# Opening the tile context of a three-block sequence kernel with its other scheduling mode

## The chip, the cores and the metric

The program runs on one core of one Trainium2 chip. The metric is the device time of one execution in microseconds; the kernel before takes 3362.69 us (median of three runs, 3362.65 to 3365.91). The engines are TensorE (PE in the profile; its weight loads are PEld), VectorE (DVE), ScalarE (ACT), GpSimd (POOL) and SyncE (SP); each works through its own list of instructions, and semaphores order what the engines hand to each other.

## What is computed

Three blocks on a sequence of 512 tokens by 1024 channels, in fp32, one after the other, and each has a mixer and a feed-forward part. Cut to what matters:

```python
# block 1: four branches, gated and merged
y_sc   = (sc_b * causal_dwconv(sc_c * sc_x, sc_conv)) @ sc_out
y_pool = pool_mixer(pool_in, pool_w, pool_scale)
y_conf = conformer_conv(conf_in, ...)
y_diff = diff_attention(q, k, v, ...) @ diff_out
x = x + (sum of sigmoid(gate_b) * y_b) @ w_o
x = x + conv_glu_ffn(rms_norm(x, ffn_norm), ffn_up, ffn_conv, ffn_down)
# block 2: adaptive norms, gated delta rule (8 heads of 64) and RWKV-7 (8 heads of 64)
y_a = gated_deltanet(qkv, z, b, a, ...) @ w_branch_gdn
y_b = rwkv7_time_mix(p_b, ...)          @ w_branch_rwkv
x = x + gate1 * ((sigmoid(gl_a) * y_a + sigmoid(gl_b) * y_b) @ w_out)
x = x + gate2 * conv_glu(norm2(x), w_ffn_in, conv_ffn, w_ffn_out)
# block 3: adaptive norms, gated linear attention and a state-space scan, both in
# both directions, with states from a context of 256 tokens; then a SwiGLU
```

## The kernel before

The activations lie feature-major: a tile is 128 channels by 512 tokens, and the 1024 channels are eight such tiles. All large weights come as one stream of pieces of eight 128x128 blocks in the order of use (464 pieces). `load()` (L315 to 329) fetches a piece of 512 KB into `wr` on SP's queue and splits it into two parts for the fast fp32r product: `wh` on ScalarE (L325) and `wl` on VectorE (L326), each with three buffers. The activations `h` are split in the same way, so that one product of 128 channels is three matmuls of 128x512 for each 128 input channels: L364 (`h` high by `wh`), L365 (`h` low by `wh`) and L366 (`h` high by `wl`) in `lin()`; L350 to L352 in `product()` do the same for halves of the tokens and for the context. `lin()` accumulates in one of three PSUM banks with the tag `mm` (L243), and a bank comes free when its result has been read.

Who runs when is not written out by hand. Python traces the program once; a scheduler in the tile context sets the order of each engine's instructions from the traced order, the dependences and priorities. `z.first()` (L252 to 254) lifts what it holds by an offset of 4000 places: the weight loads and the steps that read a product out of its bank stand under it. So the weight products, which depend on nothing but the stream, lie between the steps of the recurrences.

The mixer of block 2 (`second()`) goes over four pairs j of heads. A pair's preparation takes r, k, v and q, k, v (made by `lins(j)`) through norms (`rstds()`: L602 logarithms and L605 exponentials, each with its own table load on ScalarE; sums by L613/L614), decays (L1323 to L1355), products among tokens (L1366, L1474, L1482; L1464 broadcasts a row of decays by a GpSimd DMA) and an inversion by levels (`invert()`, L676 to L736, with transposes at L652). Then come the two chains of chunks `rwkv()` and `gdn()`; L1421, L1422, L1428, L1437 and L1443 carry RWKV's state from chunk to chunk; L1230 to L1240 norm the results and store them in `yo`. Traced behind a pair are `lins(j + 1)` and some gates, whose tanh goes to the DRAM tensor `gt` (L944, L945). Two, one, one and twelve of the sixteen gates are traced with pairs 0 to 3:

```python
            for _, o in zip(range((2, 1, 1, 12)[j]), gates):
                aside(z, z.lin(h, "w_in_2", (4912 + P * o if o < 8 else 3888 + P * (o - 8))), gt, o)
```

After the last pair, L425 and L426 (`split()`) make the two parts of the eight results (the last pair's directly), and sixteen products over `yr` and `yg` follow (`w_branch_rwkv_2` and `w_branch_gdn_2`, four input tiles each, the fourth from the last pair).

The mixer of block 3 (`third()`) starts with gated linear attention: scans (L1292), states (L1746, L1748), and eight levels of scores (L1772 to L1778, cuts of differences and their exponentials). Beside it the columns of the state-space part are made by `ssd_col()` (L1938); `conv4()` (L1916 to L1930) reads a product out of its bank with one ScalarE instruction and three VectorE taps (L1926), after which the bank is free. The state-space stage itself follows (L1972 to L2083).

Each block and each feed-forward starts with a norm in two halves of 256 tokens (`Rms`): the sums per token by L498, Newton steps for the inverse root (L506 to L515, rows of 128x2), the factor spread by L541, and then for each of eight tiles L558, L565 and L566, which write the parts of `h`.

The tile context is opened in one line of `kernel()`, L2107.

## Time and profile before

| | |
|---|---|
| median of the runs | 3362.69 us |
| span of the profiled execution | 3361.9 us |
| TensorE busy | 3272.1 us (97%) |
| weight loads (PEld) busy | 2720.8 us (81%) |
| VectorE busy | 2235.4 us (66%) |
| ScalarE busy | 1495.8 us (44%) |
| GpSimd busy | 100.5 us (3%) |
| DMA | 393 MB, 117 GB/s in the mean |
| stages of the span | block 1 mixer to some 580 us, feed-forward to 960; block 2 mixer to 1615, feed-forward to 2000; block 3 mixer to 2980, feed-forward to 3362 |

The profiled execution's own time differs from the median by 0.8 us. Busy time counts the records of an engine; records of TensorE overlap, since a matmul's end is modelled and the next one starts before it. In the groups, "idle before" is the time the engine waited ahead of the instructions of a group, and behind the arrow stands what ended most of it.

### The profile page before, as it was taken

The page shows a single profiled execution, that of the slowest core. Times are in us where ns is not written, and L with a number is a line of the kernel's source. Part 1 is how long each engine was busy: PE and PEld are TensorE (multiplying, and loading weights), DVE is VectorE, ACT ScalarE, POOL GpSimd, SP SyncE. Part 2 cuts the span into 40 slices and gives each one's busy share as a digit, 9 for nine tenths or more (in the row PEclk, how much of TensorE's full clock was granted, in tenths as well). Part 3 has the DMA queues.
Part 4 walks back from the last instruction along what each step waited for, and adds up shares of the span by engine and source line. Part 5 has one row for each costly group of instructions (what it writes and reads, how often), then busy time and mean ns, then how long its engine had stood idle before and what let it go on. Part 6 is the DMA issues. An engine that isn't in the chain of part 4 may idle for free. (4 is left out here: it accounts for less than half of the span.)

```text
span 3361.9 us, 46572 instructions
## 1 busy us (share of the span) xinstructions
PE 3272.1 (97%) x18165; PEld 2720.8 (81%) x18165; DVE 2235.4 (66%) x3675; ACT 1495.8 (44%) x2491; POOL 100.5 (3%) x186
## 2 busy tenths in 40 slices
PE   7999999999999999999999999999999999999998
PEld 6778888888887887887888888888877777888886
DVE  4696645976578677666886558777687896363344
ACT  6443423432346656653432334555546665232221
POOL 0000000000000000000000000000000001000000
PEclk9999999999999999999999999999999999999999
DMA  3222233654332112215457223222227567323222
GB/s 133 70 69 94 92 122 101 219 194 153 103 102 77 51 44 76 68 49 176 132 183 236 94 82 128 73 78 94 78 88 232 165 210 235 126 89 99 94 95 75
DMA packets 128317, 393.22 MB, mean 117 GB/s; under 512 B 16056, under 2 KB 23480, under 8 KB 128096
## 3 DMA queue, kind: packets, MB, share of 16 engines
q1 hardware_dynamic: 113776, 346.82, 32.1%
q0 software_dynamic: 13168, 42.36, 3.7%
q8 instruction: 143, 2.34, 0.3%
q10 hardware_dynamic: 1152, 1.05, 0.1%
q14 instruction: 78, 0.64, 0.1%
HBM read 358.44 MB, written 31.74 MB: 116 GB/s over the span
## 5 line engine op out<-in xcount | busy, mean ns | idle before, releaser
L364 PE MATMUL mm<-h,wh 128*128 128x512 f32 x2400 | 947.2, 395 | 0.8 <-ACT t L944 0.7
L365 PE MATMUL mm<-h,wh 128*128 128x512 f32 x2400 | 947.5, 395 | 0.0
L366 PE MATMUL mm<-h,wl 128*128 128x512 f32 x2400 | 946.5, 394 | 0.0
L325 ACT ACTIVATE wh<-wr 128x1024 fp32r<-128x1024 f32 x464 | 490.7, 1059 | 976.0 <-PE mm L365 700.6
L326 DVE TENSOR_TENSOR wl<-wr,wh 128x1024 fp32r<-128x1024 f32 x464 | 567.2, 1223 | 477.3 <-ACT wh L325 472.2
L364 PEld LDWEIGHTS mm<-h,wh 128*128 128x128 f32 x2400 | 452.2, 188 | 97.7 <-issue 5.4
L366 PEld LDWEIGHTS mm<-h,wl 128*128 128x128 f32 x2400 | 452.3, 188 | 97.3 <-issue 6.0
L365 PEld LDWEIGHTS mm<-h,wh 128*128 128x128 f32 x2400 | 452.3, 188 | 96.2 <-issue 5.4
L364 PE MATMUL mm<-p,wh 128*128 128x512 f32 x599 | 236.8, 395 | 0.0
L365 PE MATMUL mm<-p,wh 128*128 128x512 f32 x599 | 236.5, 395 | 0.1
L366 PE MATMUL mm<-p,wl 128*128 128x512 f32 x599 | 236.5, 395 | 0.0
L350 PE MATMUL mm<-h,wh 128*128 128x256 f32 (+1 forms) x480 | 159.8, 344 | 14.3 <-DVE t L1926 5.5
L351 PE MATMUL mm<-h,wh 128*128 128x256 f32 (+1 forms) x480 | 159.9, 338 | 1.6 <-DVE h L566 1.6
L352 PE MATMUL mm<-h,wl 128*128 128x256 f32 (+1 forms) x480 | 158.7, 335 | 0.0
L301 DVE SCALAR_TENSOR_TENSOR ac<-wa,adas,ac 128x1024 f32<-128x1024 f32 x98 | 125.4, 1280 | 23.0 <-DMA wa<-wa 22.7
L365 PEld LDWEIGHTS mm<-p,wh 128*128 128x128 f32 x599 | 112.5, 188 | 27.5 <-DVE p L426 0.8
L366 PEld LDWEIGHTS mm<-p,wl 128*128 128x128 f32 x599 | 112.5, 188 | 26.9
L364 PEld LDWEIGHTS mm<-p,wh 128*128 128x128 f32 x599 | 112.5, 188 | 26.5
L350 PEld LDWEIGHTS mm<-h,wh 128*128 128x128 f32 x480 | 93.4, 199 | 25.3 <-ACT h L565 4.3
L351 PEld LDWEIGHTS mm<-h,wh 128*128 128x128 f32 x480 | 94.9, 199 | 9.8 <-DVE h L566 2.2
L352 PEld LDWEIGHTS mm<-h,wl 128*128 128x128 f32 x480 | 94.8, 199 | 8.4
L747 DVE SCALAR_TENSOR_TENSOR f<-mm,par,f 128x511 f32<-128x511 f32 (+1 forms) x128 | 95.4, 745 | 1.1
(661 smaller groups left out, 5288.1 us busy)
## 6 DMA issues: line engine op xcount, KB each, us to landing
wr<-w SPq DMA_DIRECT2D x464, 512.0 KB, 3.5
wa<-wa SPq DMA_DIRECT2D x96, 512.0 KB, 4.3
e<-cum SPq DMA_DIRECT2D x64, 256.0 KB, 5.4
x<-x POOLq DMA_DIRECT2D x40, 256.0 KB, 4.9
s<-ecum SPq DMA_DIRECT2D x64, 128.0 KB, 4.4
cd<-t POOLq DMA_DIRECT2D x24, 256.0 KB, 2.3
gt<-t POOLq DMA_DIRECT2D x16, 256.0 KB, 2.5
fr<-gt SPq DMA_DIRECT2D x16, 256.0 KB, 2.9
```

The source lines that it names most:

```text
L301: self.V.scalar_tensor_tensor(a, raw, s[:, k, m:m + 1], a, op0=ALU.mult, op1=ALU.add)
L325: self.A.activation(hi, raw, AF.Copy)
L326: self.V.tensor_tensor(lo, raw, hi.bitcast(F32), op=ALU.subtract)
L350: self.T.matmul(ps[:, n], lhsT=wh, rhs=x[0][k][:, n], start=k == 0, stop=False)
L351: self.T.matmul(ps[:, n], lhsT=wh, rhs=x[1][k][:, n], start=False, stop=False)
L352: self.T.matmul(ps[:, n], lhsT=wl, rhs=x[0][k][:, n], start=False, stop=k == last)
L364: self.T.matmul(out, lhsT=wh, rhs=x[0][k], start=k == 0, stop=False)
L365: self.T.matmul(out, lhsT=wh, rhs=x[1][k], start=False, stop=False)
L366: self.T.matmul(out, lhsT=wl, rhs=x[0][k], start=False, stop=k == last)
L747: z.V.scalar_tensor_tensor(out[:, d:], src[:, :S - d], w[:, n - 1 - d:n - d], out[:, d:], op0=ALU.mult, op1=ALU.add)
```

## The change

The context is opened in the mode in which the scheduler plays the program in time, with durations that it assumes for each instruction, and takes at each point what can run then, instead of ordering by places and priorities alone. Comments and docstrings were taken out as well, which leaves the numbers of the lines as they were. No other line differs.

```diff
-    with tile.TileContext(nc) as tc:
+    with tile.TileContext(nc, schedule_with_timeline_sim=True) as tc:
```

The instructions are the same on every engine but ScalarE, which has 67 table loads in place of 65; their order differs. Three places show it.

GpSimd, second block, before pair 3: `gt` is the store of a gate (L945), `ga2317` and `ga2332` are pair 3's two broadcasts, `yo` the store of pair 2's results. Before:

```order
L945 DMA gt1377_7561<-t2541_12418 128x512
L1464 DMA ga2317_11565<-gd1408_7776 128x512
L945 DMA gt1377_7561<-t2546_12452 128x512
L945 DMA gt1377_7561<-t2551_12486 128x512
L945 DMA gt1377_7561<-t2556_12520 128x512
L1235 DMA yo1378_7562<-ga2203_11019 128x512
L1240 DMA yo1378_7562<-ra2230_11125 128x512
L945 DMA gt1377_7561<-t2561_12554 128x512
L1464 DMA ga2332_11621<-gd1408_7776 128x512
L945 DMA gt1377_7561<-t2566_12588 128x512
```

After:

```order
L945 DMA gt1377_7561<-t2571_12622 128x512
L945 DMA gt1377_7561<-t2576_12656 128x512
L945 DMA gt1377_7561<-t2581_12690 128x512
L945 DMA gt1377_7561<-t2586_12724 128x512
L945 DMA gt1377_7561<-t2591_12758 128x512
L1464 DMA ga2317_11565<-gd1408_7776 128x512
L1235 DMA yo1378_7562<-ga2203_11019 128x512
L1240 DMA yo1378_7562<-ra2230_11125 128x512
L1464 DMA ga2332_11621<-gd1408_7776 128x512
```

Ahead of pair 3's first broadcast stand two of the twelve gates t2536 to t2591 before (t2536 is the row above these), and all twelve after.

TensorE, second block, pair 3's preparation: `g` and `r` are small banks of the two chains, L1474 and L1482 the products among tokens, `mm` the bank of a weight product over `h` (before) or over `yr` (after, the fill of the next stage). Before:

```order
L365 MATMUL mm2562_12557<-h894_4666,wh2554_12492 128x512
L366 MATMUL mm2562_12557<-h893_4665,wl2555_12493 128x512
L1474 MATMUL g2320_11579<-fg2277_11385 128x128 x4
L1482 MATMUL g2322_11589<-fg2271_11346,fg2277_11385 128x128 x4
L364 MATMUL mm2562_12557<-h895_4667,wh2554_12492 128x512
L365 MATMUL mm2562_12557<-h896_4668,wh2554_12492 128x512
L366 MATMUL mm2562_12557<-h895_4667,wl2555_12493 128x512
L364 MATMUL mm2562_12557<-h897_4669,wh2554_12492 128x512
```

After:

```order
L1319 MATMUL r2319_11573<-q1400_7730,lx2311_11541 128x512
L365 MATMUL mm2616_12808<-fg2597_12770,wh2584_12696 128x512
L366 MATMUL mm2616_12808<-fg2596_12769,wl2585_12697 128x512
L365 MATMUL mm2622_12831<-fg2597_12770,wh2584_12696 128x512
L366 MATMUL mm2622_12831<-fg2596_12769,wl2585_12697 128x512
L365 MATMUL mm2625_12848<-fg2597_12770,wh2589_12730 128x512
L366 MATMUL mm2625_12848<-fg2596_12769,wl2590_12731 128x512
L1474 MATMUL g2320_11579<-fg2277_11385 128x128 x4
L1482 MATMUL g2322_11589<-fg2271_11346,fg2277_11385 128x128 x4
L613 MATMUL r2331_11615<-ra2329_11613,bd64r4_66 128x512
L614 MATMUL r2331_11615<-ra2330_11614,bd64r4_66 128x512
L652 MATMUL g2325_11599<-con2_64,ga2323_11595 128x128 x4
```

Between L1482 and the first L652 (g2325) stood 19 weight products; after, none, and those just ahead are the first parts of the three products over `yr`.

VectorE, third block, gated linear attention at 2450 us: L1926 are the three taps that read the bank mm3899, L1748 carries a state, L1772 to L1778 are score levels. Before:

```order
L1926 SCALAR_TENSOR_TENSOR t3905_20832<-mm3899_20768,par1_63,t3905_20832 128x254
L1748 SCALAR_TENSOR_TENSOR gs3948_20998<-gs3946_20994,sma3944_20990,a3947_20996 128x256
L1926 SCALAR_TENSOR_TENSOR t3905_20832<-mm3899_20768,par1_63,t3905_20832 128x255
L1753 TENSOR_TENSOR a3951_21004<-a3951_21004,kq3829_20213 128x512
L1926 SCALAR_TENSOR_TENSOR t3905_20832<-mm3899_20768,par1_63,t3905_20832 128x255
L1773 TENSOR_TENSOR a3955_21014<-a3940_20977 128x4x64
L1774 TENSOR_TENSOR a3956_21015<-a3922_20931 128x4x64
L1929 SCALAR_TENSOR_TENSOR t3905_20832<-t3906_20833,t3905_20832 128x256
```

After:

```order
L1926 SCALAR_TENSOR_TENSOR t3905_20832<-mm3899_20768,par1_63,t3905_20832 128x254
L1772 TENSOR_TENSOR a3965_21137<-a3922_20931 128x128x2
L1773 TENSOR_TENSOR a3965_21137<-a3940_20977 128x128x2
L1778 TENSOR_TENSOR a3959_21059<-a3959_21059,kq3829_20213 128x512
L1778 TENSOR_TENSOR a3960_21060<-a3960_21060,kq3827_20211 128x512
L1778 TENSOR_TENSOR a3961_21085<-a3961_21085,kq3829_20213 128x512
L1778 TENSOR_TENSOR a3962_21086<-a3962_21086,kq3827_20211 128x512
L1778 TENSOR_TENSOR a3963_21111<-a3963_21111,kq3829_20213 128x512
L1926 SCALAR_TENSOR_TENSOR t3905_20832<-mm3899_20768,par1_63,t3905_20832 128x255
L1778 TENSOR_TENSOR a3964_21112<-a3964_21112,kq3827_20211 128x512
```

The first two taps stood two rows apart; now seven rows of the score levels stand between them.

## Rows read from the trace of the kernel before

**Rows 1.** The page: the span; busy us, share and instructions by engine.

```profile
span 3361.9 us, 46572 instructions
...
PE 3272.1 (97%) x18165; PEld 2720.8 (81%) x18165; DVE 2235.4 (66%) x3675; ACT 1495.8 (44%) x2491; POOL 100.5 (3%) x186
```

**Rows 2.** Timeline of TensorE at 450 us: start, duration, engine, line, operation.

```profile
450.24 0.39 PE L364 MATMUL mm<-h,wh 128*128 128x512 f32 x1
450.47 0.39 PE L365 MATMUL mm<-h,wh 128*128 128x512 f32 x1
```

**Rows 3.** The same at 1450 us, behind a run of small matmuls.

```profile
1450.21 0.48 PE L366 MATMUL mm<-h,wl 128*128 128x512 f32 x1
1450.53 0.40 PE L364 MATMUL mm<-h,wh 128*128 128x512 f32 x1
```

**Rows 4.** Stretches: length, busy us of PE, PEld, DVE, ACT, POOL, clock, DMA.

```profile
1392.00:1452.00 60.00, 59.63 (x304) 47.30 (x304) 45.34 (x82) 40.03 (x62) 5.39 (x10) 1.00 0.37 123
1149.00:1200.00 51.00, 48.67 (x229) 39.19 (x227) 40.50 (x67) 31.73 (x50) 1.61 (x3) 1.00 0.31 98
1508.00:1531.00 23.00, 19.83 (x92) 14.98 (x91) 13.59 (x24) 15.36 (x20) 1.08 (x2) 1.00 0.28 83
2429.00:2459.00 30.00, 28.77 (x167) 24.75 (x168) 25.00 (x47) 14.09 (x26) 3.24 (x6) 1.00 0.26 90
2000.00:2030.00 30.00, 25.51 (x148) 22.79 (x147) 27.49 (x101) 14.26 (x26) 0.00 (x0) 0.89 0.21 69
400.00:500.00 100.00, 100.00 (x437) 81.53 (x436) 52.07 (x68) 36.59 (x47) 3.71 (x7) 1.00 0.35 114
2535.00:2800.00 265.00, 260.36 (x1570) 196.77 (x1569) 232.47 (x356) 183.34 (x429) 11.88 (x22) 0.99 0.64 200
```

**Rows 5.** Groups of TensorE, 1392 to 1452 us: count, busy us, mean ns, idle.

```profile
L365 PE MATMUL mm<-h,wh 128*128 128x512 f32 x58 | 23.1, 398 | 0.0
```

**Rows 6.** The timeline of TensorE again, at both ends of that stretch.

```profile
1392.04 0.39 PE L1422 MATMUL r<-vz,ra 128*128 128x128 f32 x2
1392.27 0.61 PE L1428 MATMUL r<-ra,cra 128*128 128x128 f32 x4
...
1451.75 0.60 PE L652 MATMUL r<-con,ra 128*128 128x128 f32 x4
```

**Rows 7.** Groups of ScalarE in 1392 to 1452 us.

```profile
L602 ACT ACT_TABLE_LOAD x3 | 3.8, 1283 | 0.1
...
L605 ACT ACTIVATE cga<-cga 128x1024 f32<-128x1024 f32 x2 | 2.1, 1056 | 0.0
```

**Rows 8.** Groups of VectorE in 1392 to 1452 us.

```profile
L1286 DVE TENSOR_TENSOR ra<-ra,ra 128x512 fp32r<-128x512 f32 x4 | 2.7, 687 | 3.0 <-ACT ra L1285 3.0
L1478 DVE SCALAR_TENSOR_TENSOR ga<-g,q,ga 128x128 f32<-128x128 f32 x8 | 2.4, 343 | 0.0
```

**Rows 9.** Waits of TensorE over the span: us in total, times, longest.

```profile
PE aux L498 <- DVE f L488: 12.2, 4, 8.4
PE aux L541 <- DVE f L539: 10.2, 5, 4.2
PE mm L350 <- DVE t L1926: 5.5, 6, 2.4
```

**Rows 10.** Groups of VectorE in 2210 to 2500 us.

```profile
L1778 DVE TENSOR_TENSOR a<-a,kq 128x512 f32<-128x512 f32 x42 | 28.2, 685 | 0.7 <-ACT a L1777 0.6
...
L1775 DVE TENSOR_TENSOR a<-a 128x256 f32<-128x256 f32 x21 | 8.8, 418 | 0.0
```

**Rows 11.** Another stretch at the start of block 3.

```profile
2004.00:2011.00 7.00, 6.66 (x32) 6.69 (x33) 6.10 (x28) 2.94 (x6) 0.00 (x0) 0.54 0.22 75
```

**Rows 12.** Groups of VectorE in 2000 to 2030 us.

```profile
L558 DVE SCALAR_TENSOR_TENSOR f<-x,smf,aux 128x256 f32<-128x256 f32 x16 | 7.4, 475 | 0.7 <-PE aux L541 0.7
L566 DVE SCALAR_TENSOR_TENSOR h<-f,mod,h 128x256 fp32r<-128x256 f32 x16 | 7.4, 480 | 0.0
```

## The prediction

> **What bounds the kernel now.** The page's first part comes first: TensorE is busy for 3272.1 of 3361.9 us, VectorE 66%, ScalarE 44% [rows 1]. So TensorE idles 89.8 us in all, and an order of work can give back no more than that plus what is lost inside the busy time. Inside it little is lost: in a stretch without any wait, 128x512 matmuls start every 0.22 to 0.23 us, though each record lasts 0.39 [rows 2]; 0.227 is what one costs, and a change between such products and small ones costs about 0.09 more, since the first one after a small run starts 0.32 after its predecessor, not 0.23 [rows 3]. The table by stretches then shows where other engines come near the end of a stage [rows 4]. In 400 to 500 us TensorE is full and VectorE half used; in 2535 to 2800 VectorE runs 232.5 of 265 us, nearly a second bound; at the start of block 3 (2000 to 2030) VectorE runs 27.5 of 30 us and TensorE 25.5. Between 1392 and 1452 us, where pair 3 of the second block is prepared, TensorE is full for 59.6 of 60 us although VectorE (45.3) and ScalarE (40.0) run a long serial chain: 172 weight products of 128x512, the "fill", cover it (57 or 58 on each of three lines) [rows 4, 5]. The whole kernel is built on this: recurrences and norms are chains of VectorE and ScalarE steps with tiny matmuls, and stand beside weight products that depend on nothing. TensorE takes its instructions in order, so where the fill stands decides everything. The named waits of TensorE are short and mostly at the starts of blocks (L498, L541) or on the convolution taps of block 3 (L1926) [rows 9].
>
> **What the change does.** No instruction is added but two table loads on ScalarE; the same matmuls come in another order. It does do something: of 15,941 TensorE instructions 8,629 stand elsewhere. The feed-forward stages keep their order almost row for row; the second block's pairs, the attention of block 1 and all of block 3's mixer do not. The sum therefore goes by places where, in the new order, the work of other engines between two TensorE rows lasts longer, by the durations of rows, than the TensorE work that stands between the same two.
>
> *Fewer changes of kind.* Counted in the orders, runs of 128x512 products meet runs of small ones 676 times before and 548 times after. 128 x 0.09 = 12 us saved (ends 0 and 14).
>
> *Pair 3's preparation.* In the new order all twelve gate products that stood by for pair 3 (they end in L945's stores) are spent before pair 3's first broadcast (L1464, ga2317); before, two were, four more came ahead of the second broadcast (ga2332) and six behind it. What is left as fill are the next stage's products (mm2616, mm2622, mm2625), which need the last pair's result for their last part, hold all three banks "mm" until then, and can run only nine matmuls here. From L1422 (pair 2's last state) to the first inversion step of pair 3 (L652, r2367) a chain of 48 VectorE and 20 ScalarE instructions must run. VectorE: 0.34 for 128x128 rows (L1478), 0.68 to 0.69 for most: 28.5 us by the rows' durations [rows 8]. ScalarE: five table loads of 1.28, two L605 of 1.06, the rest 0.6 to 0.7: 18.1 us [rows 7]. Together 46.7 us. Between the same two TensorE rows stand, after the change, 31 wide matmuls (31 x 0.227 = 7.0) and some 47 small ones at about 0.2 [rows 6]: 16.6 us. TensorE waits 30 us. Before, the same stretch took from 1392.04 to 1451.75, 59.7 us [rows 6], with 172 x 0.227 = 39 us of fill in it, and hid the chain but for 2. Net **+28** (20 if a third of the chain has run ahead during pair 2's end, 33 if the fill's three weight pieces are late as well).
>
> *Pair 1's preparation* (1149 to 1200 before, TensorE 48.7 of 51 [rows 4]): 41 us of such steps against 19.3 us of TensorE work that now stands there, 22 us where some 2 were: **+20** (12 to 25). *The end of pair 3* (1508 to 1531, TensorE 19.8 of 23 [rows 4]): final norms, splits L425/L426, 18.7 us against 5.2, so 13 where 5 were: **+8** (2 to 13). The work that was moved out of these places runs in pairs 0 and 2, where TensorE was full anyway and gains nothing.
>
> *Starts of blocks and feed-forwards*, six places: VectorE makes the normalised halves with 0.48 us rows (L558, L566) [rows 12], and the second half's Newton steps (L506 to L515) queue behind more of them. At block 3 the first L566 of the second half comes 67 rows behind L539 rather than 43; 24 rows of 0.16 to 0.48 are 4 to 8 us. By the same count the six places lose 2, 3, 4, 4, 4 and 7 us more than before: **+22** (8 to 30; the waits at L498 and L541, 12.2 and 10.2 us [rows 9], are these places now).
>
> *Block 3's gated attention* (2112 to 2500). The taps L1926 free a bank for the next product. At 2429 the new order has 67 VectorE rows from L1748 to the third tap of t3905, before 35: 27 more cuts (L1772 to L1775) of 0.42 and eleven L1778 of 0.68 stand among the taps [rows 10]. That is 37 us on VectorE against 24.1 us of TensorE work, a wait of 13 to 15, where VectorE before ran 25.0 of 30 us and TensorE 28.8 [rows 4]. Four more places of the stage count 4, 5, 10 and 12 us. In all 47 against 24 by the same count in the old order: **+23** (0 to 35).
>
> *What gets better.* The state-space stage and the attention of block 1 keep VectorE's total but order it a little more evenly: **-7** (-12 to +2). And many short waits of below 3 us go, since TensorE's rows stand more often where their operands are ready: of the 89.8 us of idle time the largest ones named make up a third; I take **-20** (0 to -40), the least certain term.
>
> *The clock.* After a long wait TensorE runs at the lower of its levels for a while: 2004 to 2011 shows a granted clock of 0.54, that is nearly 1.2 GHz, behind the wait at block 3's start [rows 11]. Such a stretch of 7 us costs at most 3.2. Eight places wait longer than before; much of the lost time falls into waits anyway: **+8** (0 to 25).
>
> **Sum**, on the execution profiled: 3361.9 - 12 - 20 + 28 + 20 + 8 + 22 + 23 - 7 + 8 = 3431.9. The median of the runs is 3362.7, 0.8 above it, within the spread; I say 3432.
>
> **The rivals.** (a) *Faster.* The preparation of a pair needn't wait for the end of the pair before: if ScalarE's and VectorE's rows of pairs 1 and 3 in fact run while TensorE is still in pairs 0 and 2, the 56 us of the three pair places vanish; it decides whether the chain's first 30 us run before TensorE reaches r2250's L613. With the starts and block 3 also halved: 3361.9 - 12 - 20 - 7 + 11 + 11 = 3345. For it: VectorE is free a third of the time [rows 1]. Against it: the chain's first VectorE row (L1425) reads pair 2's last state, and both engines work their queues in order.
> For headroom the Trainium skill (Perfetto Trace Analysis, Identifying the Most-Contended Engine) says matmul busy time misleads and the weight loads' busy share should be taken. That share is 81% here, which read by itself leaves 641 us to gain. The full stretch 400 to 500 shows 81.53 for it as well [rows 4], so the trace agrees that 97% is flattering as a gauge but not that 19% is free; scaled by that row the weight loads need 2720.8 / 0.8153 = 3337 us, an estimate not far from this rival's time.
> (b) *No change.* TensorE's own work bounds the kernel, and each wait found is paid back by one that goes: 3362. For it: 97% busy. Against it: a wait where fill is missing isn't given back later.
> (c) *Much slower.* The waits add up: weight pieces (L325, L326) stand in the same queues as the chains and come late after every one, and every wait above 4 us leaves a slow stretch: +35 for block 3 rather than 23, +33 and +25 for the pairs, +25 for the clock, no small waits saved; with the end of pair 3 at +13 and the starts at +30 that is 3361.9 - 12 + 33 + 25 + 13 + 30 + 35 + 25 = 3511, or half way there, 3471.
> By the Trainium skill (TensorE: Matmul & The Clock Gate, HAM oscillation) a wait between two pieces of work makes the next one start cold; rows 11 agree for one place, and it would raise this rival's chance where many waits are long.
> That the change did nothing is excluded by the orders.
>
> **How the numbers follow.** Forecast 0.70, (a) 0.11, (b) 0.06, (c) 0.13. The terms' half-widths (7, 6, 5, 11, 17, 7, 20, 12) make 34 together, as independent terms, so the forecast alone holds 3390 to 3475. (a) and half of (c) may stay out; with (b) and (c)'s lower half the range is 3358 to 3485. A measurement here tells 0.2% (6.7 us) from no change. Faster: (a), 0.11; same: (b), 0.06; slower: the forecast and (c), 0.83.
>
> **What would show it.** Right: VectorE and ScalarE alternate alone with TensorE idle for 20 to 30 us before r2367 and some 20 us before pair 1's L652; the waits on L1926 in block 3 grow from 5.5 us to above 20; feed-forward stretches keep their length. TensorE's busy sum falls below 3272 by about ten. Wrong: if pair 3's stretch shows TensorE above 90%, or the idle time of TensorE in block 3's gated stage does not grow, the chain ran ahead and (a) holds.

## The result: 3516 us, and the profile after

The changed kernel takes **3516.4 us** (median of 4 runs, 3513.6 to 3517.8) against 3362.7 beside it: **1.0452 times as long, 95% interval 1.0440 to 1.0465**, 154 us slower. The forecast of 3432 had the direction right and less than half of the size, and the range, which ended at 3485, missed the time. It is nearest to rival (c), worked out as 3511, and in part by luck: that sum had 25 for the clock, nothing for the state-space end and nothing for small waits that go, where +56, +25 and -21 were found.

The page of after, span and busy time by engine, to be read against [rows 1]:

```profile
span 3515.4 us, 46584 instructions
...
PE 3314.5 (94%) x18165; PEld 2766.9 (79%) x18165; DVE 2243.2 (64%) x3675; ACT 1491.7 (42%) x2493; POOL 101.8 (3%) x186
```

TensorE's busy time didn't fall by ten, as forecast; it grew by 42 us with the same 18165 instructions. The mean granted clock goes with it: at the lower level a product's record lasts some 0.77 us instead of 0.39, as the wait kernels below show. Span and clock of the core, in after:

```profile
core 0: 3515.4 us, clock 0.966
```

The same of before:

```profile
core 0: 3361.9 us, clock 0.993
```

At a level of one half (1.2 of 2.4 GHz), (1 - 0.966) x 3515.4 = 120 us of full-speed time were not granted, where (1 - 0.993) x 3361.9 = 24 were before. The trace's record of the clock has nine stretches at 0.50 before, 48.6 us together, and 29 after, 238.7 us, from 3.4 to 20.5 us long. Some of that falls into waits, where it costs nothing.

The longest waits of TensorE in after, to be read against [rows 9]: what it waited for, us in total, times, longest.

```profile
PE aux L541 <- DVE f L539: 26.2, 9, 5.4
PE mm L364 <- DVE a L1663: 17.8, 1, 17.8
PE mm L350 <- DVE t L1926: 17.4, 13, 5.1
PE r L613 <- ACT ra L1285: 12.4, 9, 3.7
...
PE a L652 <- DVE a L1720: 8.7, 2, 6.2
```

Two of these hardly stand in the kernel before: one wait of 17.8 us at the end of the state-space stage (L1663, none before), and waits of the attention's own chain (L1720, 0.6 us before). Stretches of after, with the columns of [rows 4]: pair 3's preparation, pair 1's, and the end of the state-space stage.

```profile
1487.00:1531.00 44.00, 27.02 (x89) 17.62 (x89) 32.68 (x63) 26.76 (x38) 2.16 (x4) 0.61 0.15 42
1210.00:1250.00 40.00, 27.61 (x113) 20.03 (x112) 30.50 (x56) 26.18 (x42) 1.85 (x3) 0.72 0.23 65
2937.00:2956.00 19.00, 1.18 (x5) 0.73 (x4) 5.76 (x8) 5.97 (x8) 5.35 (x10) 0.60 0.84 293
```

In pair 3's 44 us TensorE has 89 records where [rows 4] show 304 in 60 us at a clock of 1.00, and those 89 run at 0.61.

To see where the 154 us went, each pair of neighbouring matmuls was given the median start-to-start time of its kind in before; what exceeds it by more than 0.15 us counts as a wait, what exceeds it inside a stretch at half clock, up to its own length, as lost to the clock, and what is left as small gaps:

| us | before | after | difference |
|---|---|---|---|
| the order at its usual pace | 3170.3 | 3155.9 | -14 |
| waits | 82.2 | 214.8 | +133 |
| lost to the clock | 17.1 | 73.4 | +56 |
| small gaps | 76.4 | 55.2 | -21 |

What counts as a kind decides some of this: other ways to tell kinds apart give +115 to +143 for the waits, +53 to +59 for the clock, -15 to -21 for the gaps and +3 to -28 for the order, which is the least certain line.

By stage, from landmarks that both orders have: block 2's mixer and its end +73, block 3's from its start through its state-space stage +54, the starts of block 2 and of two feed-forwards together +21, block 1 with the first feed-forward's start -2, the rest +8.

### The profile page after: what moved, and what is told of

Read it like the earlier page. It is cut to its first block, busy times and chain, and to the rows that moved or that the text cites. A ratio compares the mean times of both kernels' runs of the same rounds, so it can differ in the third digit from the quotient of the medians.

```text
span 3515.4 us, 46584 instructions
## 1 busy us (share of the span) xinstructions
PE 3314.5 (94%) x18165; PEld 2766.9 (79%) x18165; DVE 2243.2 (64%) x3675; ACT 1491.7 (42%) x2493; POOL 101.8 (3%) x186
## 5 line engine op out<-in xcount | busy, mean ns | idle before, releaser
L364 PE MATMUL mm<-h,wh 128*128 128x512 f32 x2400 | 953.4, 398 | 31.5 <-DVE a L1663 17.8
L325 ACT ACTIVATE wh<-wr 128x1024 fp32r<-128x1024 f32 x464 | 491.0, 1059 | 1136.4 <-PE mm L365 770.1
L326 DVE TENSOR_TENSOR wl<-wr,wh 128x1024 fp32r<-128x1024 f32 x464 | 567.5, 1224 | 495.5 <-ACT wh L325 478.3
L364 PEld LDWEIGHTS mm<-h,wh 128*128 128x128 f32 x2400 | 455.3, 190 | 133.0 <-issue 27.8
L366 PEld LDWEIGHTS mm<-h,wl 128*128 128x128 f32 x2400 | 455.2, 190 | 99.3 <-issue 5.7
L365 PEld LDWEIGHTS mm<-h,wh 128*128 128x128 f32 x2400 | 455.5, 190 | 97.0 <-issue 5.3
L364 PE MATMUL mm<-p,wh 128*128 128x512 f32 x599 | 236.5, 396 | 0.0
L350 PE MATMUL mm<-h,wh 128*128 128x256 f32 (+1 forms) x480 | 168.3, 357 | 27.1 <-DVE t L1926 13.1
L351 PE MATMUL mm<-h,wh 128*128 128x256 f32 (+1 forms) x480 | 168.4, 354 | 15.1 <-DVE h L566 9.9
L352 PE MATMUL mm<-h,wl 128*128 128x256 f32 (+1 forms) x480 | 166.3, 349 | 0.0
L301 DVE SCALAR_TENSOR_TENSOR ac<-wa,adas,ac 128x1024 f32<-128x1024 f32 x98 | 124.9, 1281 | 27.8 <-DMA wa<-wa 27.1
L366 PEld LDWEIGHTS mm<-p,wl 128*128 128x128 f32 x599 | 112.5, 188 | 27.1
L364 PEld LDWEIGHTS mm<-p,wh 128*128 128x128 f32 x599 | 112.6, 188 | 26.3
L350 PEld LDWEIGHTS mm<-h,wh 128*128 128x128 f32 x480 | 99.7, 211 | 42.4 <-issue 12.8
L351 PEld LDWEIGHTS mm<-h,wh 128*128 128x128 f32 x480 | 100.5, 210 | 27.0 <-DVE h L566 12.1
L352 PEld LDWEIGHTS mm<-h,wl 128*128 128x128 f32 x480 | 100.6, 210 | 9.3
L2057 ACT ACTIVATE e<-e,tok 128x128 f32<-128x128 f32 x256 | 80.1, 391 | 42.6 <-DMA e<-cum 41.2
```

The lines of the kernel that those rows point to most:

```text
L301: self.V.scalar_tensor_tensor(a, raw, s[:, k, m:m + 1], a, op0=ALU.mult, op1=ALU.add)
L325: self.A.activation(hi, raw, AF.Copy)
L326: self.V.tensor_tensor(lo, raw, hi.bitcast(F32), op=ALU.subtract)
L350: self.T.matmul(ps[:, n], lhsT=wh, rhs=x[0][k][:, n], start=k == 0, stop=False)
L351: self.T.matmul(ps[:, n], lhsT=wh, rhs=x[1][k][:, n], start=False, stop=False)
L352: self.T.matmul(ps[:, n], lhsT=wl, rhs=x[0][k][:, n], start=False, stop=k == last)
```

## The experiments

Each changed one thing, but for the last three groups. Ratios are to the kernel before, in the same comparison.

### What one wait costs: `w6`, `w16`, `w40`

The kernel before, with six lone waits in the last feed-forward (m is 6, 16 or 40):

```
+def stall(z, ps, m):
...
+    with z.first(3 * HP):
+        t = z.tile("f", 256)
+        z.V.tensor_scalar(t, ps[:, :256], 1.0, None, op0=ALU.mult)
+        for _ in range(m):
+            z.V.tensor_scalar(t, t, 1.0, None, op0=ALU.mult)
+        return z.T.matmul(z.bank("aux")[:, :1], lhsT=t[:, :P], rhs=z.ones[:, 0:1], start=True, stop=True).ins
...
+                    with self.tc.issue_after(hold) if hold is not None else ExitStack(): g, u = [self.lin(h, *w) for w in up(j)]
```

> The kernel before, with six waits of TensorE put into the last FFN of block 3 (3041 to 3317 us, where TensorE has no wait and a granted clock of 1.00), some 30 us apart: each holds the next product behind a chain of seven 128x256 steps on VectorE that starts from the product before (0.28 to 0.48 us a step by the rows of this kernel, so 2 to 4 us, and a little for the way there and back). It measures what a single wait costs with what it does to the clock. Theory (a short wait costs only itself): +15 to +25 us, granted clock 1.00 all along the FFN. Rival (any wait is followed by a stretch at half clock): +35 or more and stretches at 0.5 to 0.6.

> The same six waits with seventeen steps each, 5 to 8 us and the way there and back. Theory (a single wait of this length leaves a stretch at half clock behind, and each costs some 3 to 6 us over its own length): the six waits sum to 36 to 50 us and the kernel is 55 to 85 us longer. Rival (the half clock comes only after waits that stand in a row, as in block 2, and a lone wait has no price but its length): the kernel is longer by the sum of the six waits, within 4 us, and the granted clock stays above 0.95 between them.

> The same six waits with forty-one steps each, 12 to 20 us. Theory: the price over its own length is that of the shorter waits again, 3 to 6 us for each, because the slow stretch behind a wait has its own length whatever the wait was: the sum of the waits and 18 to 36 us. Rival (the price grows with the wait): over 8 us for each. Second rival (no price): within 4 us of the sum of the waits.

Measured: 3410.99 us (1.0146, 1.0129 to 1.0163), 3430.49 (1.0205, 1.0189 to 1.0220) and 3473.69 (1.0338, 1.0323 to 1.0354), against 3361.86. TensorE's wait on the added chain in w6 (us in total, times, longest):

```profile
PE aux L2124 <- DVE f L2123: 27.6, 6, 4.7
```

The same in w16:

```profile
PE aux L2124 <- DVE f L2123: 47.3, 6, 7.9
```

And in w40:

```profile
PE aux L2124 <- DVE f L2123: 94.5, 6, 15.8
```

| | longer by | the six waits | left, for each wait |
|---|---|---|---|
| w6 | 49.1 | 27.6 | 3.6 |
| w16 | 68.6 | 47.3 | 3.6 |
| w40 | 111.8 | 94.5 | 2.9 |

The times are medians and the waits those of the profiled runs. In the profiled runs alone, where TensorE has the order of the kernel before but for the added matmuls, the last feed-forward is longer by 48.4, 64.3 and 112.8 us, which leaves 3.5, 2.8 and 3.0 us for each wait; w16 and w40 lose 4 to 5 us more ahead of it.

The second wait of w6 in TensorE's timeline (start, duration, operation, in brackets the wait):

```profile
3055.34 0.39 PE L366 MATMUL mm<-h,wl 128*128 128x512 f32 x1
3060.30 0.59 PE L2124 MATMUL aux<-con,f 128*128 128x1 f32 x2 [4.57 <-DVE f L2123]
3060.74 0.77 PE L364 MATMUL mm<-h,wh 128*128 128x512 f32 x1
```

The stretches around it, in the columns of [rows 4]: with the chain, behind it, and the next.

```profile
3054.80:3059.50 4.70, 0.93 (x5) 0.42 (x3) 3.67 (x8) 1.58 (x2) 0.00 (x0) 1.00 0.19 58
3059.50:3066.30 6.80, 6.00 (x15) 4.85 (x16) 0.67 (x3) 0.00 (x0) 0.00 (x0) 0.50 0.18 66
3066.30:3073.00 6.70, 6.70 (x31) 5.48 (x30) 1.82 (x2) 1.54 (x2) 0.00 (x0) 1.00 0.12 12
```

At the end of a wait of 4.6 us the clock is at 0.50, 1.2 GHz, and it stays there for 6.8 us: 15 records where the next 6.7 us have 31, and a product's record lasts 0.77 instead of 0.39. The low level begins 0.8 us before the wait ends (3059.5 and 3060.3); the 6.0 us of it that come after cost about half, 3.0, and that with the added matmul (0.4) is the price. For w6 the theory (a short wait costs only itself) fell and the rival held, though the waits were 4.6 us, not the 2 to 4 expected. For w16 the theory held, and for w40 within a us (17.3 over the six waits, where 18 to 36 were expected): the low stretches there last 6.8 to 10.2 and 17.1 us, but they begin earlier in the wait, and the price doesn't grow. One of w40, TensorE's timeline at the end of the wait:

```profile
3088.47 0.59 PE L2124 MATMUL aux<-con,f 128*128 128x1 f32 x2 [15.72 <-DVE f L2123]
```

The stretch that is low from before that end:

```profile
3077.10:3094.20 17.10, 5.73 (x15) 4.58 (x16) 10.15 (x35) 0.00 (x0) 0.00 (x0) 0.50 0.04 17
```

Only 5.7 us of it come after the wait. So **a lone wait of 4.6 to 16 us costs its own length and some 3 us more** (2.8 to 3.6). This price can't be multiplied by the 20 more low stretches of after: those last from 3.4 to 20.5 us, and some lie in waits. What they cost there is the 56 us of the table. By the Trainium skill (TensorE: Matmul & The Clock Gate, HAM oscillation) waits between bursts of matmuls, for transfers in its example, make each next burst start slow, with some 1.67 us of throttled time; the traces of the wait kernels agree on the fact, and measure 6.8 us for the time.

### The fill of block 2: `b_gates`, `e1_hold`, `e8_pace`

First the harm alone, in the old mode: the kernel before with the gate products given out so that pair 3 has none.

```
-            for _, o in zip(range((2, 1, 1, 12)[j]), gates):
+            for _, o in zip(range((6, 5, 5, 0)[j]), gates):
```

> The kernel before, in its own scheduling mode, with one thing changed: block 2's sixteen gate products are given out to the four pairs as 6, 5, 5 and 0 instead of 2, 1, 1 and 12, so that pair 3 has no product to fill TensorE with, as in the changed kernel (there 9 of the products' matmuls stand in each of the two steps between the pair's L1366 rows, where before had 139 and 55). Theory (what makes pair 3 wait is that the fill is gone, however it was spent): +25 to +60 us, TensorE's waits in pair 3's stretch 20 us or more and granted clocks of 0.7 to 0.9 there. Rival (the order of the chain's own steps is what costs, and the fill is not needed): under +10 us.

Measured: 3388.75 us, 1.0077 (1.0062 to 1.0092): +26.9. That is the harm at pair 3's preparation and at its end together, for which the prediction had +28 and +8, and it has the clock in it. TensorE's longest waits from 1430 to 1600 us in it:

```profile
PE mm L364 <- ACT ra L425: 7.2, 1, 7.2
PE r L1366 <- DVE ra L1348: 6.6, 1, 6.6
```

Two of its stretches, one in the preparation and one at the end, both at half clock throughout, where before has a clock of 1.00 [rows 4]:

```profile
1454.00:1478.00 24.00, 15.53 (x61) 12.45 (x62) 17.98 (x36) 8.16 (x17) 0.00 (x0) 0.50 0.00 1
1539.40:1556.50 17.10, 6.68 (x12) 3.76 (x13) 9.29 (x15) 8.42 (x12) 0.00 (x0) 0.50 0.12 38
```

So fill that is spent early costs time whichever mode spends it, and here somewhat less than was worked out. The mirror image, in the changed kernel, holds the fill of each pair back until the pair's own norm sums are on TensorE's queue:

```
+            mark = last_pe(z); V.tensor_tensor(kk, kk, rn[0], op=mult)
...
+            with z.tc.issue_after(mark):
+                now = lins(j + 1) if j < 3 else None
+                for _, o in zip(range((2, 1, 1, 12)[j]), gates):
```

> The changed kernel with one thing undone: in block 2 the products traced behind pair j (the next pair's and the gates) may not be issued on TensorE before the norm sums of pair j's own preparation. Theory (the fill is spent a pair too early, and the preparations of pairs 1 and 3 stand bare): the mixer of block 2, 542 us after the change and 477 before, falls below 500, its stretches at half clock from 76 us to under 20, the whole to 3465-3480. Rival (the chains themselves are ordered worse on VectorE and ScalarE, wherever the fill stands): the mixer stays above 525 and the whole above 3500.

Measured: 3500.71 us, 1.0405 (1.0389 to 1.0420), 16 back of the 36 to 51 expected, and still above the 3500 that its rival had: that the chains' own order costs too isn't excluded by this run. Pair 3's preparation is full again, pair 1's isn't, and pair 2's is now starved in the same way. Its stretches, in the order pair 3, 1, 2:

```profile
1450.00:1500.00 50.00, 49.90 (x238) 39.53 (x237) 35.41 (x57) 33.23 (x45) 5.38 (x10) 1.00 0.42 142
...
1210.00:1250.00 40.00, 29.34 (x191) 25.71 (x190) 28.84 (x56) 20.39 (x47) 0.54 (x1) 0.79 0.11 34
1350.00:1380.00 30.00, 19.49 (x133) 17.61 (x134) 21.80 (x42) 15.43 (x34) 0.54 (x1) 0.77 0.17 59
```

TensorE's longest waits from 1210 to 1380 us in it:

```profile
PE r L1366 <- DVE ra L1348: 12.6, 2, 6.3
```

Once let go, the fill is again used up in the first steps. Then it seemed that it should be spread, each product behind a place of its own in the pair's chain:

```
+            z.pace = paced(z, n0, (9, 8, 8, 12)[j])
...
+def lin_paced(z, *a, **k):
+    pace = getattr(z, "pace", None)
+    with z.tc.issue_after(pace.pop(0)) if pace else ExitStack():
+        return lin_plain(z, *a, **k)
```

> The changed kernel; the one difference: in block 2 each of the 9, 8, 8 or 12 products that fill TensorE beside a pair is held behind its own place in the pair's chain, evenly from the pair's norm sums to its end, instead of all of them behind the norm sums as in the kernel that gave 3500.7. Theory (the waits are where the fill is gone, so fill that is spread takes them away with the half clock behind them): block 2's mixer falls from 542 to 480 to 505 us, the kernel to 3455 to 3485. Rival (the chain's steps are themselves in a worse order, and fill only hides a part): no better than 3495.

Measured: 3555.57 us, 1.0572 (1.0557 to 1.0588), 39 slower than the changed kernel: a plain miss. The products that were spread are also the next pair's inputs. TensorE waited for the next pair's norms (L613 on L1285, 26.1 us in 1000 to 1680 against 12.7 in after) and its first broadcasts (L1474 on L1226, 13.3 against 7.2). That these inputs came late is read from the waits and not tested apart; if so, fill here has two uses, and the even order serves neither.

### The loads of the state-space end: `e2_ga`

```
-        for o in range(8):
-            a = z.tile("a")
-            z.nc.sync.dma_start(a, ga[:, o * S:o * S + S])
+        acc = [z.tile("a") for o in range(8)]
+        for o, a in enumerate(acc):
+            mark = z.nc.sync.dma_start(a, ga[:, o * S:o * S + S]).ins
+        for o, a in enumerate(acc):
+            with z.tc.issue_after(mark):
```

> The changed kernel with the eight loads of gates at the end of block 3's mixer (L1662) issued on SP's queue ahead of the last weight pieces instead of behind three of them. Theory (these loads queue behind weight pieces that wait for buffers): the single wait of 17.8 us of TensorE on L1663 falls to 6-10 us, the whole to 3503-3509. Rival (the loads wait for the memory of the stage before, or the fill is simply used up there): the wait stays within 2 us of 17.8 and the whole at 3514-3518.

Measured: 3508.78 us, 1.0430 (1.0414 to 1.0446), 7.6 faster, inside the theory's bounds and yet no proof of it. The wait on L1663 is gone, and another stands in its place, TensorE's longest there:

```profile
PE mm L364 <- ACT wh L325: 15.5, 1, 15.5
```

The weight pieces themselves weren't late: SP issued three from 2925.6 us on, and pieces land there within 8.4 us. Their split L325 stood on ScalarE behind splits of the stage's own results (L425), which waited for the loads `x<-ob`. ScalarE's timeline in e2_ga:

```profile
2941.89 1.97 ACT L425 ACTIVATE ys<-x 128x512 fp32r<-128x512 f32 x3 [8.86 <-DMA x<-ob]
2944.28 0.63 ACT L425 ACTIVATE ys<-x 128x512 fp32r<-128x512 f32 x1 [0.42 <-DMA x<-ob]
2944.82 2.94 ACT L325 ACTIVATE wh<-wr 128x1024 fp32r<-128x1024 f32 x3
```

In after the transfers are 84% busy there at 293 GB/s (the last stretch row above), and TensorE has nothing left to do beside them.

### The gated attention: `e3_gla`, `g1_pace`

The same two holds for the products beside the heads of block 3's attention: all behind the head's first matmul, or spread over its chain.

```
+                n0 = len(z.nc.cur_bb.bb.instructions); z.run(gla(z, c, j, *now, yd))
+                with z.tc.issue_after(last_pe(z, n0)):
...
+                z.pace = paced(z, n0, 4 * (j < 3) + FA[j] + FC[j])
```

> The changed kernel with the products that are traced behind head j of block 3's gated attention held on TensorE until the first matmul of head j. Theory (the same early spending of fill makes the 34 us of this stage): 477 us of the stage fall to 455 or less, the whole to 3490-3497. Rival (the taps L1926 that free the banks stand behind score levels on VectorE, whatever TensorE's order): the stage stays at 470-480 and the waits on L1926 at 15-20 us.

> The changed kernel; the one difference: the products that fill TensorE beside the gated attention of block 3 (six columns for each head, and the next head's own products) are each held behind a place of its own in the head's chain, evenly, instead of running as soon as a bank is free. Theory (dense fill makes TensorE wait for the taps L1926 that free its two banks, and leaves nothing for the chain's steps): the stage falls from 477 to 445 to 462 us, the kernel to 3486 to 3502. Rival (the taps' place behind other steps of VectorE and ScalarE is what costs, however the products stand; holding all of them behind the head's first matmul gave +15): within 8 us of the changed kernel, or worse.

Measured: 3531.04 us (1.0492) and 3537.78 (1.0513, 1.0497 to 1.0529), both slower than the changed kernel, by 15 and 21, which of the theories and rivals only g1_pace's rival allowed; in both the waits of L652 on L1720 grew from 8.7 us to over 20, while those of L350 on L1926 fell from 17.4 to 11.3 and 13.2. Holding the products back doesn't mend this stage. The trace of after shows how such a wait comes about, at 2401 to 2409 us: VectorE's timeline.

```profile
2401.24 1.76 DVE L1698 SCALAR_TENSOR_TENSOR y<-y,y 128x1536 f32<-128x1536 f32 x1 [2.67 <-ACT y L1697]
...
2404.13 1.22 DVE L326 TENSOR_TENSOR wl<-wr,wh 128x1024 fp32r<-128x1024 f32 x1 [0.25 <-ACT wh L325]
2405.27 0.68 DVE L1715 TENSOR_TENSOR_SCAN a<-con,y 128x256 f32<-128x256 f32 x1
...
2407.48 0.41 DVE L1720 TENSOR_TENSOR a<-a,u 128x256 f32<-128x256 f32 x1
```

TensorE's, at the end of it:

```profile
2407.95 0.69 PE L652 MATMUL a<-con,a 128*128 128x128 f32 x2 [6.16 <-DVE a L1720]
2408.70 0.76 PE L350 MATMUL mm<-h,wh 128*128 128x512 f32 x1
```

TensorE stands 6.16 us at a transpose of the chain; of the 40 matmuls queued behind it 33 are products. The step was placed as if its input were there; it came late because VectorE first waited for ScalarE (L1697), and then did a weight piece (L326).

### The starts: `e4_into`, `s1_sums`

Two halves of one suspicion: VectorE's norm steps kept as traced (L558 to L566), or TensorE's sums for the second half of the tokens (L498) put ahead of the products of the first.

```
+                i = z.V.tensor_tensor(lo, t, hi.bitcast(F32), op=ALU.subtract); z.tc.keep_in_program_order(i)
...
-                self.product(p, ws, x, n)
+                with self.tc.issue_after(self.sums): self.product(p, ws, x, n)
```

> The changed kernel with VectorE's steps of the norm at the start of a block or feed-forward (L558 to L566) kept in the order in which they are traced. Theory (at these starts the second half's Newton steps and L566 are late because VectorE takes other rows first): the five starts, each 6.4 to 7.8 us longer than before, lose 5 us each, the whole goes to 3485-3495. Rival (the rows of the other half are needed anyhow, and the low clock after the first wait makes the difference): 3510 or more.

> The changed kernel; the one difference: where a stage starts on the first half of the tokens (L374), its products wait on TensorE's queue behind the norm sums of the second half (L498), which stand before them in the kernel before and behind some 25 products in the changed one. Theory (at the starts TensorE's order keeps the second half's norm steps from running beside the first half's splits): -10 to -25 us against the changed kernel (3491 to 3506), the wait of VectorE for L498 at the last FFN's start gone. Rival (the starts are longer because of VectorE's and ScalarE's own orders): within 5 us of the changed kernel (3511 to 3521).

Measured: 3514.14 us (1.0448, 1.0431 to 1.0466), nothing, as the rival had it; and 3510.05 (1.0434, 1.0419 to 1.0450), 6 of the 10 to 25 expected, between what theory and rival allowed. With the sums first, TensorE waits at them. VectorE's timeline in s1_sums at the second feed-forward's start:

```profile
1697.85 2.43 DVE L558 SCALAR_TENSOR_TENSOR f<-x,mod,aux 128x256 f32<-128x256 f32 x6
1700.20 1.22 DVE L326 TENSOR_TENSOR wl<-wr,wh 128x1024 fp32r<-128x1024 f32 x1
1701.33 0.42 DVE L488 TENSOR_TENSOR f<-f,f 128x256 f32<-128x256 f32 x1
1701.67 2.46 DVE L566 SCALAR_TENSOR_TENSOR h<-f,mod,h 128x256 fp32r<-128x256 f32 x6
1704.05 0.15 DVE L524 TENSOR_SCALAR nw<-aux 128x2 f32<-128x2 f32 x1
```

The same place in the kernel before:

```profile
1613.90 0.87 DVE L558 SCALAR_TENSOR_TENSOR f<-x,mod,aux 128x256 f32<-128x256 f32 x2
1614.83 0.42 DVE L488 TENSOR_TENSOR f<-f,f 128x256 f32<-128x256 f32 x1
1615.23 0.89 DVE L566 SCALAR_TENSOR_TENSOR h<-f,mod,h 128x256 fp32r<-128x256 f32 x2
...
1617.25 0.16 DVE L506 TENSOR_SCALAR nw<-nw 128x2 int32<-128x2 int32 x1
```

Before, the second half's last square (L488) comes after two L558, and its Newton steps run between the first half's splits. The new mode does six L558, a weight piece, L488, six L566 and only then L524: nothing of the second half is hidden. Either engine's repair leaves the other's order in the way.

### Three edits together: `e9_three`

The spread fill of e8_pace, the loads of e2_ga and the sums of s1_sums.

> The changed kernel with three edits together: the fill of block 2 spread evenly, the eight loads of the gates ahead of the weight pieces at the end of the state-space stage (alone 3508.8), and the products of a stage's start behind the second half's norm sums. Theory (they lie in different stages and add up): the changed kernel's 3516 less the gains of each alone, 3430 to 3470, within 6 us of that sum. Rival (what one gains shows up as a wait of another, since the weight pieces and the clock tie the stages together): a third or more of the sum of the gains is missing.

Measured: 3547.60 us, 1.0549 (1.0532 to 1.0567). Added up, the three alone give 3516.4 + 39.1 - 7.6 - 6.4 = 3541.5; so they add, within 6 us, but on a sum with the wrong sign.

### Whose order it is: `p_pe`, `p_va`, `p_pd`, `p_all`

Repairs of single places hadn't settled it. These four kernels keep the changed kernel's mode and hold whole engines to the order that they have in the kernel before, by an ordering edge from each instruction of the engine to the one that stood ahead of it; the other engines are ordered by the new mode around that.

```
-            whole(z, out)
+            whole(z, out); as_before(tc, PE)
...
+def as_before(tc, *tables):
...
+            if last is not None:
+                tc.add_manual_dep(at[f"I-{n}"], last, mybir.DependencyInfo(mybir.DependencyClass.NoSync, mybir.DependencyReason.DATA), reason="as before")
+            last = f"I-{n}"
```

> The changed kernel's scheduling mode, but with every instruction of TensorE held to the order that it has in the kernel before (all 14644 rows stand alike); VectorE, ScalarE and the queues are ordered by the new mode around that. Theory (the loss sits in TensorE's order: products spent early, chain steps set ahead of products that were ready, second-half sums late): at least two thirds of the 154 us come back, 3345 to 3410 us, and TensorE's waits in block 2's mixer and in the gated attention fall to within 15 us of the kernel before. Rival (VectorE and ScalarE carry the loss, and the chains come late whatever TensorE's order is): 3440 or more.

> The mirror image: the changed kernel's scheduling mode with all of VectorE's and ScalarE's instructions held to the order of the kernel before (3542 and 2338 rows alike), and TensorE and the queues ordered by the new mode around that. Theory (the loss sits in TensorE's order): 3450 or more. Rival (it sits in VectorE's and ScalarE's): 3420 or less, with the waits of the gated attention and of the starts as in the kernel before.

> The same with TensorE and VectorE held to their order in the kernel before, and ScalarE ordered by the new mode. Theory (the waits that TensorE's old order meets are on VectorE's lines, L1926, L1014, L539, L488, L2059, so it is VectorE's order that has to fit): 3390 or less. Rival (ScalarE's order, with its changes of kind taken away, keeps VectorE's steps waiting): 3450 or more.

> The changed kernel's scheduling mode with all three engines, TensorE, VectorE and ScalarE, held to their order in the kernel before; only the queues that issue transfers are left to the new mode (168 lines of difference on SP). Theory (an order of one engine costs when it doesn't fit the others': 3531 with TensorE's alone, 3713 with the other two alone): 3355 to 3375. Rival (SP's order of loads carries a part): 3390 or more.

| order of before on | us | ratio and interval |
|---|---|---|
| none (the changed kernel) | 3516.4 | 1.0452 (1.0440 to 1.0465) |
| TensorE (p_pe) | 3530.9 | 1.0503 (1.0488 to 1.0519) |
| VectorE, ScalarE (p_va) | 3712.7 | 1.1044 (1.1025 to 1.1062) |
| TensorE, VectorE (p_pd) | 3436.4 | 1.0219 (1.0203 to 1.0234) |
| all three (p_all) | 3367.1 | 1.0010 (1.0001 to 1.0019) |

With all three as before, the time of before is back to 4 us, so the edges cost next to nothing and the transfers' queues, still ordered by the new mode, carry nothing of weight. But the loss belongs to no engine. TensorE's old order alone is worse than the new one, where the theory wanted two thirds back, and the other two alone are far worse, where the rival wanted 3420; with two of the three the time lies between what theory and rival gave. By their numbers p_pe's rival (the loss is VectorE's and ScalarE's) and p_va's theory (it is TensorE's) are both met, and they contradict each other: a run that takes over one side alone can't tell whose the loss is. TensorE's longest waits in p_pe:

```profile
PE mm L350 <- DVE t L1926: 27.8, 13, 8.0
PE tp L1017 <- DVE a L1014: 22.2, 7, 7.4
```

And in p_pd:

```profile
PE mm L350 <- DVE t L1926: 13.0, 5, 7.4
PE aux L498 <- DVE f L488: 12.2, 4, 8.4
```

The stages, in us between landmarks (the first matmul of the same tile) that all six have:

| | before | after | p_pe | p_va | p_pd | p_all |
|---|---|---|---|---|---|---|
| block 1's mixer to FFN 1's first product | 586.9 | 584.5 | 628.8 | 664.3 | 586.8 | 586.6 |
| block 2's mixer and its end | 555.4 | 628.4 | 589.0 | 710.7 | 576.4 | 557.2 |
| block 3's start to its state-space end | 844.6 | 898.4 | 907.1 | 948.0 | 889.8 | 843.8 |
| of this, the state-space end | 25.2 | 50.0 | 25.2 | 30.8 | 27.1 | 25.2 |
| starts of FFN 2 and FFN 3 | 130.3 | 144.9 | 139.2 | 136.7 | 131.4 | 130.2 |

The wait at the state-space end is gone with TensorE's old order, with the loads still ordered by the new mode; but VectorE's and ScalarE's old orders alone take most of it too (30.8 us, where 25.2 and 50.0 are the ends). So it hangs on how the orders meet, and isn't one engine's. Taken over one after the other, the shares are these, and they would differ in another succession. Of block 2's 73 us TensorE's old order brings back 39, VectorE's on top 13, ScalarE's 19. In block 3 TensorE's order brings back the 25 at the state-space end and loses 34 elsewhere; VectorE's then gives 17, ScalarE's 46. In block 1, where the new mode has no loss, TensorE's old order among new ones makes one of 42 us, and VectorE's and ScalarE's one of 77.

### Taking only the gains: `h1`, `h2`

The table of p_all without the instructions of block 1's mixer, and without those of the state-space stage too:

> Held to the order of the kernel before on TensorE, VectorE and ScalarE, except for block 1's mixer, which the new mode orders (there the changed kernel took 551.4 us against 556.5). Theory (the new mode's gain in a stage where TensorE doesn't wait can be had by itself): 3352 to 3361, 2 to 8 us under the kernel before. Rival (the gain is lost where the old order takes over, at the first FFN's start): 3361 or more.

> The same with block 3's state-space stage left to the new mode too (there 298.8 us against 305.6, but a wait of 17.8 at its end). Theory (the end keeps the old order and has its loads in time, as with TensorE's old order alone, where that wait was gone): 3344 to 3356. Rival (the stage's orders don't fit those before and behind it): 3362 or more.

Measured: 3361.58 us, 0.9993 (0.9984 to 1.0002), and 3369.28, 1.0016 (1.0007 to 1.0025). In h1's profiled run block 1's mixer takes 552.5 us against 556.5, so the gain is there, but the median can't be told from no change. Its nearer base is p_all, with the same mode and the same orders elsewhere: against that it is 5 us faster, about what block 1's mixer gives, so the gain seems to come through, and what holding the orders costs takes it away again. In h2 the state-space stage takes 308.4 us between its landmarks against 305.6 before, and its end 30.6 against 25.2. The 298.8 of the changed kernel had been cut by the count of matmuls, since its order runs some of them on the other side of the landmark; either that gain was one of the cut, or it doesn't travel. No kernel here beats the kernel before by a measurable amount.

## Why the prediction was wrong, point by point

In the terms of the table of waits and clock, the forecast had +94 for the waits (28 + 20 + 8 + 22 + 23 - 7), +8 for the clock, -20 for small gaps and -12 for the order; +133, +56, -21 and -14 were found. Two terms fell short, the clock by 48 us and the waits by 39.

**The mechanism and the direction** were right: chains of VectorE and ScalarE steps lie bare where the fill that stood beside them is gone. b_gates takes the fill of pair 3 alone and loses 26.9 us, clock included, where 28 and 8 were forecast. In after block 2 has +73 where the three pair places had 56; some 30 of the 73 are the clock. Pair 3's chain has the length that was worked out, 46.1 us from pair 2's last L1422 (1484.95) to pair 3's first L652 on `r` (1531.02), for 46.7. The sign named for it came only in part: TensorE idles 17.0 of pair 3's 44 us, not 20 to 30, and 12.4 of pair 1's 40, not some 20, because its few matmuls there run at 0.61 and 0.72 of the clock.

**The clock was the largest miss**: +8 forecast (0 to 25), some 56 found. The step that failed stands in the text: "Eight places wait longer than before", at "at most 3.2" each. The size was right for a lone wait, some 3 in the three wait kernels. The number of places was wrong, 20 more low stretches and not eight, and so was their length, up to 20.5 us and not 7. The count took long waits alone, by a misreading of [rows 11]: the two waits ahead of that low stretch are short. TensorE's timeline there, in the kernel before:

```profile
2002.48 0.67 PE L541 MATMUL aux<-f,con 128*128 128x256 f32 x2 [1.58 <-DVE f L539]
...
2004.34 0.78 PE L498 MATMUL aux<-con,f 128*128 128x1 f32 x4 [1.19 <-DVE f L488]
```

In after a low stretch stands at a single wait of 2.9 us, the only one from 2426 to 2443 us:

```profile
2436.37 2.08 PE L1764 MATMUL a<-kq,kq 128*128 128x128 f32 x8 [2.90 <-DVE gs L1748]
```

The stretch, in the columns of [rows 4]:

```profile
2435.70:2442.50 6.80, 6.13 (x40) 5.17 (x41) 5.73 (x12) 1.50 (x3) 0.61 (x2) 0.50 0.10 39
```

That lost time falls into waits was right for a part only: of the 96 us more that weren't granted some 40 did, and 56 fell on matmuls that would have run at full speed. The sign in the profile was wrong too: TensorE's busy sum rose by 42 us.

**The state-space end** had no term: 25.2 us became 50.0, with one wait of 17.8. The orders showed SP with three weight pieces ahead of the eight loads L1662; I took the stage for a gain because I costed its VectorE steps, and neither its transfers nor the products that had stood beside them.

**Block 3's attention**: +23 forecast (0 to 35). Its waits on L1926 grew from 5.5 to 21.1 us (17.4 before L350, 3.7 before L364), as foretold in sum, though the one wait of 13 to 15 us at the tap of t3905 isn't there: thirteen waits, the longest 5.1, make up the 17.4. Attention and state-space stage together are 28 longer between landmarks; cut by the count of matmuls, +33 and -7. The term held in size, and its excess is the clock (+14 there); of its cause, the taps, 15.6 us are found, and the rest stands at other lines, L1720 with 8.1 more among them.

**The starts**: +22 forecast (8 to 30), 25 to 36 found, by where a start is cut, some 12 of it the clock.

**The gains**: -12 for fewer changes of kind came as -14, -20 for small gaps as -21, and block 1's part of the -7 as -5 (551.4 us against 556.5). They were right as the table tells kinds apart, and stand in a sum that the other terms decide. The half-widths were too narrow: a place was left out, and the terms weren't independent, since the clock's price lies on many of their waits at once.

Rival (a) falls with pair 3's 27.0 of 44 us. Rival (c) named what decided, many slow stretches behind waits, and got 0.13; its condition, "every wait above 4 us", is too narrow by the rows just shown, and its 3511 is partly luck, as said at the start. What the rule of the Trainium skill cited there says, that a wait makes the next work start cold, was borne out by the wait kernels.

**What stays open.** How much of block 3's loss outside the state-space end is a chain step set too early on TensorE, and how much a step of VectorE or ScalarE set too late, was not separated further than the table above; an order by the new mode with other durations was not tried. Of the starts, a repair of TensorE's and VectorE's orders together was not tried without the rest.

## What to carry to other kernels

Price a wait of an otherwise full TensorE at its length plus the half-speed stretch behind it (some 3 us here, for lone waits of 4.6 to 16 us), and count the places first, short waits among them: here low stretches stood at waits of 1.6 and 2.9 us too, for which no price was measured. Orders of engines are one thing: a tuned order taken over for one engine alone can cost more than none, so compare kernels by whole orders, and check a repair by whether the wait is gone, not by whether the time fell. Fill has a place as well as an amount; fill that was somebody's input too gave back 16 us here when it was held back whole, and cost 39 when it was spread.

## What the hardware showed unexpectedly

A lone wait of 4.6 us in a stretch with no other wait took TensorE to 1.2 GHz for 6.8 us, six times out of six, and one of 15.7 us cost no more than that one beyond its own length. A wait of 2.9 us with no other near it was met by the same 6.8 us once, so a short wait isn't safe by being short.
